# A decoder layer on one core: the FFN's down-projection by Strassen's seven products, in three batches of the contraction

## The chip, the cores and the metric

The kernel runs on one core of a Trainium2 chip. Times are device microseconds (us) of one execution. The profile is that of one execution, taken by the hardware profiler. Engines: PE (TensorE, matmuls), PEld (its weight loads), DVE (VectorE), ACT (ScalarE), POOL (GpSimd), SP (SyncE, which only issues DMAs here). SPq, ACTq and so on are the queues from which DMAs and semaphore instructions are issued.

## What is computed

A decoder layer with retention, differential attention and a gated MLP, on 1024 positions and 16 meta tokens, model width 1024, FFN width 2816, float32. Only its end is touched:

```python
    u = rmsnorm(h, norm2_w[l])
    up = causal_dwconv(u @ w_up[l].astype(dt), conv_w[l], conv_b[l])
    a, b = jnp.split(up, 2, axis=-1)
    h = h + (jax.nn.silu(a) * b) @ w_down[l].astype(dt)
```

w_up is 1024 x 5632, w_down 2816 x 1024. All is kept transposed: channels on the 128 partitions, positions along a row.

## The kernel before

Every matmul is done in float32r with both operands split: h is a cast to float32r on ACT, l the rest (x - h) by a subtraction. A product is three matmuls, (wh, xh), (wh, xl), (wl, xh), written out in product() (L1186). The subtractions are put in a list by low_later() and written out on DVE by lows() (L1138) a few steps later; those of the weights whose name stands in self.pooled go to POOL (L1144).

From last_ret_out on, the program is recorded by hand: each engine runs its instructions in the order of the code. What an engine waits for, all behind it on the engine waits for too.

**Up-projection.** It already goes by Strassen's algorithm in Winograd's form. Block f (0 to 21; NF = 22) makes the rows f (part a) and NF + f (part b) of the up-projection, for 1032 positions in two halves of 516. The seven products are named A F B E H G D, in that order on PE; each runs over four row tiles of 128, in two pieces of 258 columns, into one double bank of PSUM (four double banks in turn). B is added to A's bank, D to E's. Around them: A is copied by ACT (L1716), A + B too (L1730); DVE forms "sw" (L1625, after F), "su" (L1631, after H), mid() (L1635, which reads E's bank before D adds to it), and the results ub (L1640, after G) and ua (L1645, after D). The weights of the products come from five loads of 256 KB (s1 s3 a b d), two of them completed by an adding DMA on POOL (L1549) and two sums on DVE ("S" L1556, "T" L1558); seven casts and subtractions make the operands for block f + 1 during block f, in the order A, S F, B, H, E, T G, D.

**Activation.** Behind block f come, two blocks later, the convolution and the gate: ACT starts it (L1594), DVE adds the taps (L1600, four for each part), ACT does Silu (L1603), DVE multiplies twice (L1605), and SP stores the 128 x 1024 result to DRAM (L1607).

**Down-projection.** Eleven passes of two row tiles each; a pass reads two activations back (L1799), splits them (ACT L1806, DVE L1138), and for each of eight row tiles m of the output does two products of 1024 columns in two banks. DVE adds the bank to the residual h[m] in SBUF (L1787), which in the last pass goes out in halves (L1789):

```python
                self.product([(ps[:, :512], 0, 512), (ps[:, 512:], 512, 512)], [(w(o + i), (gh[i], gl[i])) for i in range(2)])
                for cs in [slice(0, 512), slice(512, SEQ)] if last else [slice(0, SEQ)]:
                    V.tensor_add(h[m][:, cs], h[m][:, cs], ps[:, cs])
```

The residual lies in DRAM (self.hs) before and is loaded at the end of block 21. Large tiles come from one pool of 34 (big()).

## Time and profile before

| | |
|---|---|
| median of 3 runs | 2491.41 us (2488.54 to 2492.39) |
| profiled execution, its own time | 2491.43 us |
| its span (first to last instruction) | 2489.7 us |
| busy: PE, DVE, ACT, POOL | 2447.4, 1705.7, 1041.8, 431.1 us |
| clock granted to PE, mean | 0.999 |
| HBM read, written | 199.55 MB, 58.12 MB |

A row of the trace groups equal instructions that follow each other: start, length, engine, line, operation, tiles, count, and in brackets how long the engine was idle before and what ended that. The length of a group of x2 or x4 is from the first start to the last end; neighbours overlap a little, so I go by the spacing of starts. Numbers of buffers are left out of the names: u is ua, d a bank of PSUM, wr a raw tile of weights, wh and wl its two parts, b a large tile.

### The profile page before, as it was taken

The page shows a single profiled execution, that of the slowest core. Times are in us where ns is not written, and L with a number is a line of the kernel's source. Part 1 is how long each engine was busy: PE and PEld are TensorE (multiplying, and loading weights), DVE is VectorE, ACT ScalarE, POOL GpSimd, SP SyncE. Part 2 cuts the span into 40 slices and gives each one's busy share as a digit, 9 for nine tenths or more (in the row PEclk, how much of TensorE's full clock was granted, in tenths as well). Part 3 has the DMA queues.
Part 4 walks back from the last instruction along what each step waited for, and adds up shares of the span by engine and source line. Part 5 has one row for each costly group of instructions (what it writes and reads, how often), then busy time and mean ns, then how long its engine had stood idle before and what let it go on. Part 6 is the DMA issues. An engine that isn't in the chain of part 4 may idle for free. (4 is left out here: it accounts for less than half of the span.)

```text
span 2489.7 us, 42767 instructions
## 1 busy us (share of the span) xinstructions
PE 2447.4 (98%) x16186; PEld 2355.1 (95%) x16186; DVE 1705.7 (69%) x3625; ACT 1041.8 (42%) x2106; POOL 431.1 (17%) x412
## 2 busy tenths in 40 slices
...
DMA packets 193582, 279.82 MB, mean 112 GB/s; under 512 B 29160, under 2 KB 111712, under 8 KB 193376
## 3 DMA queue, kind: packets, MB, share of 16 engines
...
HBM read 199.55 MB, written 58.12 MB: 103 GB/s over the span
## 5 line engine op out<-in xcount | busy, mean ns | idle before, releaser
L180 PE MATMUL acc<-b,wh 128*128 128x342 f32 (+2 forms) x4672 | 1122.2, 323 | 5.2 <-DVE ev L630 3.7
L180 PEld LDWEIGHTS acc<-b,wh 128*128 128x128 f32 x4672 | 802.9, 189 | 7.3 <-issue 4.0
L180 PE MATMUL acc<-b,wl 128*128 128x342 f32 (+2 forms) x2336 | 749.4, 321 | 0.0
L1186 PE MATMUL d<-b,wh 128*128 128x258 f32 (+3 forms) x3936 | 732.0, 305 | 8.5 <-DVE b L1138 3.3
L1186 PEld LDWEIGHTS d<-b,wh 128*128 128x128 f32 x3936 | 585.4, 189 | 41.5 <-DVE b L1138 4.5
L1186 PE MATMUL d<-b,wl 128*128 128x258 f32 (+3 forms) x1968 | 440.3, 305 | 2.4 <-POOL wl L1144 1.4
L180 PEld LDWEIGHTS acc<-b,wl 128*128 128x128 f32 x2336 | 441.2, 189 | 0.0
L1186 PEld LDWEIGHTS d<-b,wl 128*128 128x128 f32 x1968 | 318.7, 189 | 19.1 <-POOL wl L1144 2.6
L1142 ACT CAST wh<-wr 128x512 fp32r<-128x512 f32 x246 | 144.4, 616 | 164.9 <-DVE wr L1556 79.4
L1144 POOL TENSOR_TENSOR wl<-wr,wh 128x512 fp32r<-128x512 f32 x84 | 114.9, 1385 | 512.0 <-ACT wh L1142 498.0
L233 ACT CAST wh<-wr 128x512 fp32r<-128x512 f32 x192 | 113.3, 618 | 172.8 <-PE acc L180 157.2
L630 DVE TENSOR_TENSOR ev<-acc,b 128x342 f32<-128x342 f32 (+2 forms) x141 | 72.2, 513 | 157.3 <-PE acc L180 149.9
L1787 DVE TENSOR_TENSOR b<-b,d 128x1024 f32<-128x1024 f32 (+1 forms) x96 | 107.3, 1129 | 73.7 <-PE d L1186 71.1
L719 ACT ACTIVATE b<-b,sm 128x272 f32<-128x272 f32 (+7 forms) x128 | 101.1, 790 | 107.3 <-DVE sm L718 84.0
L711 DVE CUSTOM_DVE_ANT_0 b<-sc,consts 128x144 f32<-128x144 f32 (+6 forms) x224 | 105.9, 504 | 42.2 <-PE sc L180 41.2
L252 POOL TENSOR_TENSOR b<-b,b 128x512 fp32r<-128x512 f32 x64 | 86.2, 1348 | 209.2 <-ACT b L247 180.9
L234 DVE TENSOR_TENSOR wl<-wr,wh 128x512 fp32r<-128x512 f32 x154 | 105.6, 703 | 22.1 <-ACT wh L233 22.0
L247 ACT CAST ah<-sc 128x512 fp32r<-128x512 f32 (+2 forms) x144 | 67.3, 468 | 115.5 <-PE sc L736 92.9
L1138 DVE TENSOR_TENSOR wl<-wr,wh 128x512 fp32r<-128x512 f32 x162 | 106.9, 684 | 10.4 <-ACT wh L1142 10.4
L252 DVE TENSOR_TENSOR al<-sc,ah 128x512 fp32r<-128x512 f32 (+2 forms) x144 | 77.3, 538 | 44.8 <-ACT ah L247 43.9
L596 POOL TENSOR_TENSOR sh<-sh,b 128x346 f32<-128x346 f32 (+1 forms) x42 | 43.3, 1032 | 354.6 <-DVE sh L594 354.6
L180 PE MATMUL sc<-b,b 128*128 128x346 f32 (+9 forms) x528 | 103.2, 316 | 0.1
...
## 6 DMA issues: line engine op xcount, KB each, us to landing
wr<-w_in SPq DMA_DIRECT2D x164, 256.0 KB
wr<-w_up SPq DMA_DIRECT2D x118, 256.0 KB
...
b<-d SPq DMA_DIRECT2D x256, 64.0 KB
...
wr<-w_up POOLq DMA_DIRECT2D x44, 256.0 KB, 4.7
```

The source lines that it names most:

```text
L180: self.E.matmul(out, lhsT=l, rhs=r, start=start, stop=stop)
L233: self.A.copy(h, raw)
L234: (self.G if el == "G" else self.V).tensor_sub(l, raw, h.bitcast(F32))
L252: (self.V if el == "V" else self.G).tensor_sub(dl, src, dh.bitcast(F32))
L630: V.tensor_mul(o[:, :n], ps[:, :n], self.rb[:, cs])
L711: V.tensor_tensor_reduce(out=sc_[:m, a0:a0 + sz], in0=ps[:m, :sz], in1=mk, scale=1.0, scalar=3e38, op0=ALU.add, op1=ALU.min, accum_out=sm[ ...
L719: A.activation(sc_[:m, :n], sc_[:m, :n], AF.Exp, bias=mx, scale=-1.0, accum_out=sm[:m, 10 + c:11 + c])
L1138: self.V.tensor_sub(l, x, h.bitcast(F32))
L1142: self.A.copy(w[0], raw)
L1144: self.G.tensor_sub(w[1], raw, w[0].bitcast(F32))
L1186: self.E.matmul(o[:, :n], lhsT=l, rhs=x[:, t0:t0 + n], start=f, stop=e, skip_group_check=more)
L1787: V.tensor_add(h[m][:, cs], h[m][:, cs], ps[:, cs])
```

## The change

The down-projection goes by the same seven products. The 22 row tiles of the contraction are taken in three batches of 8, 8 and 6; a batch is four blocks (22 to 25, 26 to 29, 30 to 33) that run in the loop of the up-projection's blocks, with 4, 4 and 3 row tiles per product and halves of 512 positions. Each block gives two of the output's eight row tiles.

keep() takes the place of the activation's store: from each activation it makes what the seven operands A, H, E, F, G or B, D, F, G, H need (one subtraction on DVE, in the second half of a batch also a negation on ACT) and writes it to DRAM, five transfers of 256 KB; what two activations give together is added by the transfer (issued from POOL), the rest is stored from ACT's queue. One block before a batch begins, fetch() loads the operands from ACT's queue, one after each product (forms(0) to forms(6)), in two tiles of 1024 columns (1024 and 512 in the last batch), and two steps later finish() casts each tile on ACT and puts its subtraction in DVE's list. The blocks of the first two batches add their two rows to the residual in DRAM by adding transfers from POOL (add()); those of the last batch load it (rows()), add it on DVE and store the output.

```diff
+    def stage_of(f): return 0 if f < NF else 1 + (f - NF) // 4
+    @staticmethod
+    def tiles_of(f): return 3 if f >= NF + 8 else 4
+    def pair_of(self, f):
+        if f < NF:
+            return self.a["w_up"][f], self.a["w_up"][NF + f]
+        i = 8 * ((f - NF) // 4) + (f - NF) % 4
+        return self.a["w_down"][i], self.a["w_down"][i + 4]
...
+    def keep(self, f, o, x):
+        s, n = 1 + f // 8, 3 if f >= 16 else 4
+        k, second = (f - 8 * (s - 1)) % n, f - 8 * (s - 1) >= n
+        lo, hi, a, b = o[:, :512], o[:, 512:SEQ], x[:, :512], x[:, 512:SEQ]
+        if second:
+            self.V.tensor_sub(a, hi, lo)
+            self.A.activation(b, hi, AF.Copy, scale=-1.0)
+        else:
+            self.V.tensor_sub(a, lo, hi)
+        for name, t in zip(*(("BDFGH", (lo, hi, hi, a, b)) if second else ("AHEFG", (lo, hi, a, a, a)))):
+            if (s, name) not in self.part:
+                self.part[s, name] = self.dram([P, 2048])
+            d = self.part[s, name][:, 512 * k:512 * k + 512]
+            if second and name in "FGH":
+                self.nc.gpsimd.dma_start(out=d, in_=t, accum_op=ALU.add)
+            else:
+                self.A.dma_start(out=d, in_=t)
+    def fetch(self, name, f):
+        s, n = self.stage_of(f), 512 * self.tiles_of(f)
+        cs = [slice(0, 1024), slice(1024, n)]
+        self.coming[name] = [self.big()[:, :c.stop - c.start] for c in cs]
+        for t, c in zip(self.coming[name], cs):
+            self.A.dma_start(out=t, in_=self.part[s, name][:, c])
+    def finish(self, name, f):
+        out = self.ops[self.stage_of(f), name] = []
+        for t in self.coming.pop(name):
+            h, l = self.big(F32R), self.big(F32R)
+            c = slice(0, t.shape[1])
+            self.A.copy(h[:, c], t)
+            self.low_later(l[:, c], t, h[:, c])
+            out.append((h, l))
+            self.lows(1)
...
     def quad_product(self, ps, f, name, more=False):
         w = self.wq[f].pop(name)
-        outs = [(ps[:, 512 * g:512 * g + 512], t0, n) for g, (t0, n) in enumerate(self.PIECES)]
-        self.product(outs, [((w[0][:, k, :], w[1][:, k, :]), self.xs(name, k)) for k in range(4)], not more, True, more)
+        outs = [(ps[:, 512 * g:512 * g + 512], t0, n) for g, (t0, n) in enumerate(self.PIECES if f < NF else [(0, 512)])]
+        self.product(outs, [((w[0][:, k, :], w[1][:, k, :]), self.xs(name, k, f)) for k in range(self.tiles_of(f))], not more, True, more)
...
-            self.acts.append(self.dram([P, SEQ]))
-            self.S.dma_start(out=self.acts[f], in_=o[0][:, :SEQ])
+            self.keep(f, o[0], o[1])
...
+        def add(f):
+            m = (f - NF) % 4
+            for t, r in ((ua[f], m), (ub[f], m + 4)):
+                self.nc.gpsimd.dma_start(out=self.hs[r][:, 8:], in_=t[:, :SEQ], accum_op=ALU.add)
+        def rows(f):
+            h = [self.big() for _ in range(2)]
+            for t, r in zip(h, ((f - NF) % 4, (f - NF) % 4 + 4)):
+                self.S.dma_start(out=t[:, :SEQ], in_=self.hs[r][:, 8:])
+            return h
+        def out(f, r, t, i):
+            c = slice(512 * i, 512 * i + 512)
+            self.S.dma_start(out=self.a["out"][(f - NF) % 4 + 4 * r][:, c], in_=t[:, c])
...
+        end = NF + 12
+        for f in range(2, end):
+            pro, n = f < self.PRO, wid(f)
+            final = f >= NF + 8
+            fresh = f + 1 in (NF, NF + 4, NF + 8)
+            begun = f in (NF, NF + 4, NF + 8)
+            todo = iter([] if f == end - 1 else ["E", "HSF", "T", "GD"] if f + 1 < self.PRO else ["A", "SF", "B", "H", "E", "TG", "D"])
+            self.pooled = "EFHGD" if f + 1 < self.PRO else "BED" if f < NF - 1 else 'BEDG'
+            start, taps, mul = act.pop(f - 2) if f < NF + 2 else 3 * [lambda *a: None]
             def w():
                 self.lows()
-                for n in next(todo, ""):
-                    self.weights(f + 1, n)
+                for i in next(todo, ""):
+                    self.weights(f + 1, i)
...
+            def forms(i):
+                names = "AFBEHGD"
+                if fresh:
+                    if i > 1:
+                        self.finish(names[i - 2], f + 1)
+                    self.fetch(names[i], f + 1)
+                elif begun and i < 2:
+                    self.finish(names[i + 5], f)
             if not pro:
                 ua[f] = self.work()
-                st[f] = ua[f][:, 516:1032]
+                st[f] = ua[f][:, n:2 * n]
                 pt = self.dbl()
                 self.quad_product(pt, f, "A")
-                A.copy(bd(st[f]), d2(pt))
+                A.copy(bd(st[f]), d2(pt, f))
                 w()
                 taps(1)
-            if last:
-                self.queue = [self.a["w_down"][i] for i in range(NF)]
-                self.request()
-                self.request()
+                forms(0)
...
             up_f(f)
             if pro:
                 taps(1)
             w()
+            forms(1)
             if not pro:
                 taps(0)
                 self.quad_product(pt, f, "B", True)
-                A.copy(bd(ua[f][:, :516]), d2(pt))
+                if final:
+                    h = rows(f)
+                    V.tensor_add(ua[f][:, :512], pt[:, :512], h[0][:, :512])
+                    out(f, 0, ua[f], 0)
+                else:
+                    A.copy(bd(ua[f][:, :n]), d2(pt, f))
                 w()
-            if last:
-                self.down_fetch(0)
-            if self.PRO <= f + 2 < NF:
+            forms(2)
+            if self.PRO <= f + 2 < end:
                 self.quad_loads(f + 2)
             up_e(f)
-            if last:
-                self.arrive()
+            forms(3)
             if pro and f == 3:
                 w()
             up_h(f)
             mid(f)
+            if final:
+                V.tensor_add(ub[f][:, 512:SEQ], ub[f][:, 512:SEQ], h[1][:, 512:SEQ])
+                out(f, 1, ub[f], 1)
+                V.tensor_add(su[f], su[f], h[1][:, :512])
+                V.tensor_add(sw[f], sw[f], h[0][:, 512:SEQ])
             if pro:
                 taps(0)
             if not pro or f == 2:
@@ -1747,65 +1842,30 @@
             if f == 2:
                 w()
             mul()
-            if self.PRO <= f + 2 < NF:
+            forms(4)
+            if self.PRO <= f + 2 < end:
                 self.sum_d(f + 2)
-            if last:
-                down = self.down_split()
             w()
             up_g(f)
-            act[f - 1] = self.activation(f - 1, ua[f - 1], ub[f - 1])
-            act[f - 1][0](1)
+            forms(5)
+            if final:
+                out(f, 1, ub[f], 0)
+            if f - 1 < NF:
+                act[f - 1] = self.activation(f - 1, ua[f - 1], ub[f - 1])
+                act[f - 1][0](1)
             w()
             up_d(f)
-            act[f - 1][0](0)
+            if final:
+                out(f, 0, ua[f], 1)
+            if f - 1 < NF:
+                act[f - 1][0](0)
+            if f >= NF and not final:
+                add(f)
+            forms(6)
             w()
             for names in todo:
                 self.weights(f + 1, names)
             self.lows()
-            if last:
-                for _ in range(8):
-                    load_h()
-        h = done
-        f = NF - 1
...
-        for p in range(NF // 2):
-            gh, gl = down
...
     def down_blocks(w):
-        w = w.reshape(11, 2, P, 2, 4, P)
-        return np.ascontiguousarray(w.transpose(0, 3, 2, 4, 1, 5)).reshape(22, P, 8, P)
+        w = w.reshape(NF, P, 8, P)
+        b = np.zeros((3, 8, P, 8, P), w.dtype)
+        for i in range(2):
+            b[i] = w[8 * i:8 * i + 8].transpose(2, 1, 0, 3)
+        b[2, :, :, :3] = w[16:19].transpose(2, 1, 0, 3)
+        b[2, :, :, 4:7] = w[19:].transpose(2, 1, 0, 3)
+        return np.ascontiguousarray(b.reshape(24, P, 8, P))
```

On PE the inner pattern changes. The first matmuls of the down-projection before (x2: the two halves of a double bank with the same weights; b are the two parts of an activation):

```order
L1186 MATMUL d_26044<-b_25949,wh_25907 128x512 x2
L1186 MATMUL d_26044<-b_25950,wh_25907 128x512 x2
L1186 MATMUL d_26044<-b_25949,wl_25908 128x512 x2
L1186 MATMUL d_26044<-b_25952,wh_25907 128x512 x2
L1186 MATMUL d_26044<-b_25953,wh_25907 128x512 x2
```

and those of block 22 now:

```order
L1186 MATMUL d_26219<-b_26006,wh_25925 128x512
L1186 MATMUL d_26219<-b_26007,wh_25925 128x512
L1186 MATMUL d_26219<-b_26006,wl_25926 128x512
L1186 MATMUL d_26219<-b_26006,wh_25925 128x512
L1186 MATMUL d_26219<-b_26007,wh_25925 128x512
```

One bank of 512 columns per row tile, so every tile of weights is used for one matmul of each kind.

On ACT, before, from the Silu of block 20 to the first copy of block 21 (the copy is L1716; between are casts of weights and the start of an activation):

```order
L1603 ACTIVATE b_25542<-b_25542 128x1024
L1142 CAST wh_25713<-wr_25405 128x512
L1594 ACTIVATE b_25743<-b_25467,cols 128x512 x2
L1142 CAST wh_25747<-wr_25413 128x512
L1594 ACTIVATE b_25775<-u_25305,cols 128x512 x2
L1142 CAST wh_25779<-wr_25411 128x512
L1716 COPY u_25783<-d_25784 128x516
```

and now the same place one block later, the end of block 21 up to the first copy of block 22 (L1805); L1535 are the casts of finish() for the operands E and H, L1528 the loads of fetch():

```order
L1535 CAST b_26154<-b_26060 128x1024
L1535 CAST b_26157<-b_26061 128x1024
L1528 DMA b_26161<-d_21377 128x1024
L1528 DMA b_26162<-d_21377 128x1024
L1651 ACTIVATE b_26165<-b_25811,cols 128x512 x2
L1142 CAST wh_26170<-wr_25757 128x512
L1651 ACTIVATE b_26199<-u_25649,cols 128x512 x2
L1535 CAST b_26202<-b_26117 128x1024
L1535 CAST b_26205<-b_26118 128x1024
L1142 CAST wh_26214<-wr_25755 128x512
L1805 COPY u_26218<-d_26219 128x512
```

The copy stands behind the operands' casts; the two rows left out are further loads. Ahead of this piece stand the Silu, the negation, two stores of keep() and the casts of B.

On DVE, now, in block 22 (L1138 on b: the operands G and D, on wl: weights; L1657 the taps; L1686 "sw", L1613 "S", L1692 "su", L1697 mid()):

```order
L1657 SCALAR_TENSOR_TENSOR b_26165<-b_25811,cols,b_26165 128x512 x4
L1138 TENSOR_TENSOR wl_26234<-wr_26021,wh_26233 128x512
L1138 TENSOR_TENSOR b_26241<-b_26161,b_26240 128x1024
L1686 TENSOR_TENSOR sw_26261<-u_26218,d_26248 128x512
L1138 TENSOR_TENSOR b_26245<-b_26162,b_26244 128x1024
L1613 TENSOR_TENSOR wr_26021<-wr_26021,wr_26017 128x512
L1138 TENSOR_TENSOR wl_26266<-wr_26021,wh_26265 128x512
L1138 TENSOR_TENSOR b_26269<-b_26209,b_26268 128x1024
L1657 SCALAR_TENSOR_TENSOR b_26199<-u_25649,cols,b_26199 128x512 x4
L1138 TENSOR_TENSOR b_26273<-b_26210,b_26272 128x1024
L1692 TENSOR_TENSOR su_26334<-d_26321,sw_26261 128x512
L1697 TENSOR_TENSOR b_26336<-su_26334,d_26308 128x512
```

Before, the four subtractions of b are not there; between the two groups of taps stand "sw", a weight's subtraction and "S", and after the second group a weight's subtraction, "su" and mid().

## Rows read from the trace of the kernel before

**Rows 1.** The page's first part: busy us (share of the span) x instructions of each engine.

```profile
PE 2447.4 (98%) x16186; PEld 2355.1 (95%) x16186; DVE 1705.7 (69%) x3625; ACT 1041.8 (42%) x2106; POOL 431.1 (17%) x412
```

**Rows 2.** Busy time of the engines in stretches of 50 us: the start of the up-projection's blocks, their steady part, the down-projection. Columns: stretch, its length, busy us of PE, PEld, DVE, ACT, POOL (x instructions), granted clock of PE, busy share of the DMA engines, GB/s.

```profile
1850.00:1900.00 50.00, 46.04 (x373) 44.93 (x372) 45.33 (x56) 24.19 (x36) 20.03 (x17) 1.00 0.51 128
2150.00:2200.00 50.00, 50.00 (x418) 50.00 (x417) 36.75 (x52) 23.62 (x38) 15.55 (x14) 1.00 0.46 112
2250.00:2300.00 50.00, 50.00 (x218) 40.59 (x217) 42.46 (x48) 13.57 (x19) 0.00 (x0) 1.00 0.43 154
```

**Rows 3.** Groups of matmuls by line and shape: the two of 512 columns at L1186 (x count | busy us, mean ns of one | idle before).

```profile
L1186 PE MATMUL d<-b,wh 128*128 128x512 f32 x704 | 190.9, 392 | 0.0
...
L1186 PE MATMUL d<-b,wl 128*128 128x512 f32 x352 | 109.8, 393 | 0.0
```

**Rows 4.** PE in order of time, in the down-projection: start, length, matmuls.

```profile
2255.99 0.62 PE L1186 MATMUL d<-b,wl 128*128 128x512 f32 x2
2256.45 1.09 PE L1186 MATMUL d<-b,wh 128*128 128x512 f32 x4
2257.37 0.63 PE L1186 MATMUL d<-b,wl 128*128 128x512 f32 x2
```

**Rows 5.** The same in the input projection, where each tile of weights is used for one bank at a time.

```profile
100.16 0.32 PE L180 MATMUL acc<-b,wl 128*128 128x346 f32 x1
100.31 0.48 PE L180 MATMUL acc<-b,wh 128*128 128x346 f32 x2
100.63 0.32 PE L180 MATMUL acc<-b,wl 128*128 128x346 f32 x1
```

**Rows 6.** DVE in order of time, its last row: the two adds behind the last matmul.

```profile
2485.09 1.28 DVE L1787 TENSOR_TENSOR b<-b,d 128x512 f32<-128x512 f32 x2 [1.47 <-PE d L1186]
```

**Rows 7.** ACT in order of time, in block 20 and at the start of block 21.

```profile
2203.95 0.59 ACT L1716 COPY u<-d 128x516 f32<-128x516 f32 x1 [3.57 <-PE d L1186]
...
2212.75 1.06 ACT L1603 ACTIVATE b<-b 128x1024 f32<-128x1024 f32 x1 [1.43 <-DVE b L1600]
2213.71 0.60 ACT L1142 CAST wh<-wr 128x512 fp32r<-128x512 f32 x1
...
2216.16 1.52 ACT L1594 ACTIVATE b<-u,cols 128x512 f32<-128x512 f32 x2
2219.99 0.62 ACT L1142 CAST wh<-wr 128x512 fp32r<-128x512 f32 x1 [2.32 <-DVE wr L1558]
2224.18 0.59 ACT L1716 COPY u<-d 128x516 f32<-128x516 f32 x1 [3.57 <-PE d L1186]
2229.91 0.59 ACT L1730 COPY u<-d 128x516 f32<-128x516 f32 x1 [5.14 <-PE d L1186]
```

**Rows 8.** DVE in order of time, in block 20 and at the start of block 21.

```profile
2206.86 0.69 DVE L1625 TENSOR_TENSOR sw<-u,d 128x516 f32<-128x516 f32 x1 [1.66 <-PE d L1186]
...
2208.80 3.91 DVE L1600 SCALAR_TENSOR_TENSOR b<-u,cols,b 128x512 f32<-128x512 f32 x4
...
2215.47 0.69 DVE L1631 TENSOR_TENSOR su<-d,sw 128x516 f32<-128x516 f32 x1 [2.16 <-PE d L1186]
...
2216.81 1.29 DVE L1605 TENSOR_TENSOR b<-b,b 128x512 f32<-128x512 f32 x2
2218.02 0.68 DVE L1138 TENSOR_TENSOR wl<-wr,wh 128x512 fp32r<-128x512 f32 x1
...
2221.24 0.69 DVE L1645 TENSOR_TENSOR u<-sw,d 128x516 f32<-128x516 f32 x1 [1.34 <-PE d L1186]
...
2222.45 2.98 DVE L1600 SCALAR_TENSOR_TENSOR b<-b,cols,b 128x512 f32<-128x512 f32 x4
```

**Rows 9.** What it takes a queue to issue a DMA (SP and POOL in order of time: a load of 256 KB, a store of 512 KB twice, eight loads of 512 KB; two adding transfers of POOL), and the page's row for those adding transfers (256 KB each, median us from issue to landing).

```profile
1894.78 2.09 SPq L1128 DMA_DIRECT2D wr<-w_up  x2
1896.92 0.42 SPq L1607 DMA_DIRECT2D d<-b  x1
...
2238.39 0.32 SPq L1607 DMA_DIRECT2D d<-b  x1
2238.76 5.06 SPq L1697 DMA_DIRECT2D b<-d  x8
...
1891.17 1.83 POOL L1549 DMA_DIRECT2D wr<-w_up  x2
...
wr<-w_up POOLq DMA_DIRECT2D x44, 256.0 KB, 4.7
```

**Rows 10.** The front, blocks 2 to 4: the multiplies of the first two activations on DVE, the first copy of block 4 on ACT, and the matmul behind it.

```profile
1859.85 3.81 DVE L1605 TENSOR_TENSOR b<-b,b 128x512 f32<-128x512 f32 x2 [2.34 <-ACT b L1603]
...
1875.12 2.40 DVE L1605 TENSOR_TENSOR b<-b,b 128x512 f32<-128x512 f32 x2 [1.13 <-ACT b L1603]
...
1882.23 0.58 ACT L1716 COPY u<-d 128x516 f32<-128x516 f32 x1
...
1882.87 0.51 PE L1186 MATMUL d<-b,wh 128*128 128x258 f32 x2 [2.03 <-ACT u L1716]
```

**Rows 11.** Groups by line and shape from 2225 on: the split of one activation of 1024 columns (x count | busy us, mean ns of one | idle before).

```profile
L1806 ACT CAST b<-b 128x1024 fp32r<-128x1024 f32 x22 | 23.0, 1049 | 99.5 <-DMA b<-d 99.5
...
L1138 DVE TENSOR_TENSOR b<-b,b 128x1024 fp32r<-128x1024 f32 x22 | 26.1, 1220 | 3.0 <-ACT b L1806 2.9
```

**Rows 12.** The columns of rows 2, for 4 us in which the residual and the first activations are loaded.

```profile
2244.00:2248.00 4.00, 4.00 (x19) 3.25 (x18) 3.25 (x4) 0.00 (x0) 0.00 (x0) 1.00 1.02 418
```

109 lines of the change are left out of this document (39 added, 70 removed).

## The prediction

> **What bounds the kernel now.** The page's first part comes first: TensorE (PE) is busy 98% of the span, VectorE (DVE) 69%, ScalarE (ACT) 42% [rows 1]. An average says little, so I read the stretches. In the up-projection's steady part (2150 to 2200) and in the down-projection (2250 to 2300) PE has no idle time at all at a granted clock of 1.00, so there the time is the number of matmuls times their spacing; only around 1850 to 1900, where the up-projection starts, does PE lose 4 us in 50, with DVE at 45 [rows 2]. What the change removes from PE is therefore time, as long as nobody makes PE wait instead.
>
> **The matmuls.** Down-projection before: 704 + 352 = 1056 matmuls of 512 columns [rows 3], one group of six every 1.38 us (2255.99 to 2257.37), 0.23 us each, 242.9 us in all [rows 4]. After: twelve blocks of seven products; a product over n row tiles is 3n matmuls of 512 columns. n is 4, 4 and 3, so 4 x 7 x 3 x (4 + 4 + 3) = 924, at 0.23 us 212.5 us. Gain: 132 x 0.23 = 30.4 us. A tile of weights now serves one bank instead of two. That should cost nothing: the input projection at 100 us has the same pattern (wh, wh, wl, one bank each) and needs 0.16 us for 346 columns, 0.144 us of streaming at 2.4 GHz plus the same 0.017 us that 512 columns show over their 0.213 [rows 4, 5].
>
> **The end.** Now the last matmul is followed by two adds of 512 columns, 1.28 us [rows 6], and the output's transfer; after, by one add. I take 0.6 us off.
>
> **The steady up-projection.** A block lasts 20.23 us (one copy of product A to the next), so a product lasts 2.89 us [rows 7]. keep() gives DVE one subtraction (0.61 us by the spacing of the two multiplies) where DVE is idle over 4 us a block in waits for PE: "su", "sw" and "u" each begin on PE's time [rows 8]. Its two or five stores are on ACT, whose queue stops until DVE has multiplied. By the rows of the block that starts at 2203.95: the multiplies end at 2218.0, the subtraction at 2218.6, and five stores at 0.42 us, which is what a store of 512 KB takes on SP [rows 9], bring ACT to 2220.1. Behind them stand a cast, a pair of activations, a cast, a pair (4.0 us from 2213.71 to the end of the pair begun at 2216.16) and a last cast of 0.5, so ACT is free at 2224.6 and the copy of the next A ends at 2225.1 instead of 2224.7. PE needs it only for product B, a product after 2224.2, at 2227.1. I take nothing; the cover is 2.0 us, and each 0.1 us more per store eats 0.5 of it.
>
> **The front.** At 1882.87 PE already waits 2.03 us for just that copy, with ACT behind [rows 10]. In blocks 2 and 3 the multiplies end late (1863.6 and 1877.5), and the casts and activations that stand behind the Silu before would move behind five stores: about 2.5 us later at 1875, plus a wait for stores to land before a buffer is reused. Bounds 0 (the lag is absorbed) and 6; I take 3 us, lost for good, since PE has no idle time behind it to win back.
>
> **The first change of stage (blocks 21 and 22).** Here the down-projection's operands are made: seven, each of two tiles of 1024 columns, with a cast on ACT (0.99 us) and a subtraction on DVE (1.17 us) per tile [rows 11]; ten tiles in block 21, four in 22. DVE's block costs 36.75 / 50 of 20.23 = 14.9 us now [rows 2]; ten lows of 1.17 make 26.6 us (keep's 0.6 is paid by a low of the weights that goes to POOL). So the lag has to show somewhere, and I follow the order of the instructions on ACT and DVE, on the axis of before, where block 21 starts at 2221.3 (its copy of A at 2224.18, less a product).
> First ACT. It ends the copy of B at 2230.4 [rows 7], a cast at 2230.9, A's two at 2232.9 (0.5 and 0.99 us each). F's fetch waits behind a cast that waits for the sum S (2208.8 + 20.2 = 2229.0, where the slow taps begin [rows 8]), so it lands at about 2233.5 (some 4.5 us later, as POOL's transfers [rows 9]), F's casts end at 2235.5, then a cast and the Silu at 2237. DVE, held by two tiles' lows, does "su", the mid subtraction and another low before the multiplies, which end at 2240.6. Two stores end at 2241.4. Then, in order: two casts of B (2243.4), one weight, two of E (2245.9), a pair of activations, a weight, a pair (2249.4), two of H (2251.4), a weight, and only then the copy of block 22's first product, done at 2252.5. Product B of block 22 accumulates in the same bank and would start at 2241.4 + 2 x 12 x 0.23 = 2246.9. PE waits 5.6 us.
> Then DVE. It has H's second low at 2252.7, a pair of taps to 2255.7, then a weight's low, G, "sw", G, the weight sum S at 2259.9. ACT's next cast waits for S, so D's tiles come at 2262.4; DVE then does a low, D, the four slower taps (3.92 us [rows 8]), D, "su" and the mid subtraction, at 2268.9. Product D writes into the bank that the mid subtraction reads. PE, through with G at 2263.5, waits 5.4 us. Together 11.0 us. Lower bound 4, if tiles arrive early and DVE's taps all take 0.75 us; upper 20, if each of 14 fetches also holds ACT by 0.63 us (eight loads of 512 KB in 5.06 us on SP [rows 9]). Block 23 has no operands to make and catches up.
>
> **The other two changes of stage.** No activations run there. ACT has 5 x 2 x 0.99 + 7 x 0.52 + 1.1 = 14.6 us of work, DVE 11.7 + 3 + 3.3 = 18 us, against 19.3 us of PE. By the same walk ACT is through its chain 21.4 us after the block's start, before the copy's product ends at 22.1, and PE needs the copy at 24.8: a slack of 2.9 with the copy's 0.5. Lower bound 0. The bytes are tighter: 7.3 MB of operands, 1.8 MB of weights and 1 MB added to DRAM are 10.1 MB, 24 us at the 418 GB/s that the bursts at 2244 reach [rows 12]; but D may land in the next block. Upper bound 5 each; I take 1 each.
>
> **Hidden elsewhere.** The adding stores and the adds of the residual go out on POOL, which is busy about 15.6 of 50 us [rows 2], 0.9 us an issue [rows 9]; each block adds at most three issues, 2.7 us. No row shows an adding transfer into DRAM. The nearest is the one into SBUF (4.7 us to landing [rows 9]). What reads them comes at least three blocks (43 us) later, so between 0 and ten times that price nothing waits. More DRAM writes in the up-projection, 0.8 MB per block, add 40 GB/s to 112 [rows 2].
>
> **A rule weighed.** ACT has issued no DMA so far, so the trace can't say whether an issue stops its casts; SP's rows give only the price, 0.32 to 1 us [rows 9]. The Trainium skill (Perfetto Trace Analysis, section "DMA Instruction — HWDGE (DVE, Sync)") says that the sequencer itself waits for the semaphores and is free only when all descriptors are made; work already handed to the engine is not stopped. By that the wait for DVE in keep() holds all of ACT, as I have counted it; and the fetches are free only while ACT has a backlog. By its strict reading, with no backlog, the sum would be the second rival's.
>
> **Sum.** Against the profiled execution, 2491.43 us by its own time (span 2489.7, 1.7 us around it; the median of the runs is 2491.41): 2491.4 - 30.4 - 0.6 + 3 + 11 + 2 = 2476.4 us.
>
> **Rivals.** (1) The stage changes are hidden. For: products B and D wait only because of the queues' order, and ACT has 58% idle. Against: the walk above. 2491.4 - 31 + 0 to 8 = 2460 to 2468.
> (2) ACT's issues stand in line: each fetch of 512 KB costs ACT its 0.63 us. For: SP's loads stand back to back at that price. Against: ACT is backlogged there and should have casts handed over. Seven pairs are 8.8 us on the first change; on the others 8.8 less ACT's 2.9 of slack, 5.9 each: 2476.4 - 2 + 8.8 + 11.8 = 2495.0. It decides against the change where 42 issues less 5.8 us eat the 17 us that are left, from 0.54 us per issue; at 0.9 us, POOL's price, the changes cost 12.6 and twice 12.6 - 2.9, and the steady blocks with five stores (11 of them) lose (0.9 - 0.42) x 5 - 2.0 = 0.4 us each: 2476.4 - 2 + 12.6 + 2 x 9.7 + 4.4 = 2511.
> (3) Transfers bound the changes: operands land 5 us late at the second and third, and 3 us at the first: 2476.4 + 8 + 3 = 2487. For: 10.1 MB against 418 GB/s; against: the end of the fetch isn't needed until a block later.
> (4) The matmuls don't get 0.23 us with weights used once; then the gain shrinks by 0.9 us per ns: at 0.25 us, 2495. Against: rows 5.
>
> **How the numbers follow.** My forecast (2470 to 2483) 0.47; (1) 0.20; (2) 0.18; (3) 0.12; (4) 0.03. The predicted time is the forecast's, 2476. A measurement of this kernel tells about 0.2% (5 us) from no change, so faster ends at 2486.4: all of the forecast and (1), half of (3): 0.73. Within 0.2%, 2486.4 to 2496.4: half of (3), a part of (2) and (4): 0.14. Slower: the rest of (2): 0.13. The range 2463 to 2496 leaves out the lowest of (1) and the upper half of (2), some 0.15.
>
> **What would show it.** Right: 924 matmuls of 512 columns at 0.23 us; PE without idle time in blocks 5 to 20; a wait of PE for ACT's copy and one for DVE's mid subtraction after 2240, 4 to 8 us each, and under 3 us at the later changes. Wrong: PE waits for ACT's copies throughout (the store's price), waits of 5 us or more at the second and third change (issues or transfers), or none at the first. What would undo the forecast most is a price of ACT's issues over 0.54 us.

## The result, and the profile after

The changed kernel takes 2511.7 us (median of 4, 2509.97 to 2516.47) against 2491.9 of the kernel before beside it: ratio 1.0085, 95% interval 1.0067 to 1.0102: slower by 0.85%, clear of the spread. The forecast was 2476.4, the range 2463 to 2496. The profiled execution took 2511.67 us.

The page of the changed kernel, parts 1 and 3 (queues: packets, MB, share of the 16 engines' time), and three windows (us, busy us and instructions of PE, PEld, DVE, ACT, POOL, then granted clock, busy share of the transfer engines, GB/s):

```profile
PE 2431.2 (97%) x16054; PEld 2336.6 (93%) x16054; DVE 1737.6 (69%) x3665; ACT 1091.3 (43%) x2197; POOL 559.6 (22%) x531
q0 software_dynamic: 22608, 53.52, 12.3%
2150.00:2200.00 50.00, 49.02 (x405) 48.68 (x404) 41.73 (x55) 21.25 (x34) 18.97 (x17) 1.00 0.63 155
2250.00:2300.00 50.00, 35.21 (x133) 27.65 (x132) 41.67 (x45) 23.02 (x34) 18.94 (x17) 0.83 0.75 186
2300.00:2350.00 50.00, 41.76 (x174) 33.31 (x175) 24.17 (x30) 16.46 (x25) 21.79 (x21) 0.95 0.96 229
```

Before, PE was busy 2447.4 us [rows 1] and had no idle time from 2150 to 2200 and from 2250 to 2300 [rows 2]. Now it does less work, but stands still for 15 of the 50 us from 2250, at a granted clock of 0.83, and the transfer engines are full from 2300 to 2350 (0.96). The longest waits, from PE's timeline (in brackets how long PE stood, and for what):

```profile
1869.16 1.20 PE L1186 MATMUL d<-b,wh 128*128 128x258 f32 x4 [3.90 <-DVE b L1697]
1882.57 0.74 PE L1186 MATMUL d<-b,wh 128*128 128x258 f32 x4 [2.17 <-ACT u L1805]
2257.89 1.22 PE L1186 MATMUL d<-b,wh 128*128 128x512 f32 x2 [7.79 <-ACT u L1805]
2277.40 1.19 PE L1186 MATMUL d<-b,wh 128*128 128x512 f32 x2 [5.55 <-DVE b L1697]
2347.58 1.22 PE L1186 MATMUL d<-b,wh 128*128 128x512 f32 x2 [6.98 <-DVE b L1697]
2360.55 0.73 PE L1186 MATMUL d<-b,wh 128*128 128x512 f32 x2 [2.20 <-ACT u L1805]
2374.47 0.70 PE L1186 MATMUL d<-b,wh 128*128 128x512 f32 x2 [2.56 <-DVE b L1697]
2443.77 0.73 PE L1186 MATMUL d<-b,wh 128*128 128x512 f32 x2 [2.28 <-ACT u L1805]
2457.69 0.81 PE L1186 MATMUL d<-b,wh 128*128 128x512 f32 x2 [3.75 <-DVE b L1697]
```

L1805 is the copy of product A, L1697 the mid subtraction. The length of the group behind a wait tells the clock: a pair of 512 columns takes 0.70 to 0.73 us at full clock and 1.19 to 1.22 at the lower of its two levels, a four of 258 columns 0.74 and 1.20. So the front (the first blocks of the up-projection), the first change of stage (2257, 2277), the second (2347 to 2374) and the third (2443, 2457) all wait, not only the first change.

**The account.** I cut each trace at the copies of A and set the stretches against what PE alone needs: 19.43 us for a block of 84 matmuls (block 27 takes 19.44), so 0.2313 us per matmul. What a stretch takes beyond that is called its loss. "Front" runs from ACT's last table load, ahead of the first Silu, to the copy of block 21, less the 366.7 us of the kernel before; the three changes are blocks 21 to 23, 24 to 27, and 28 to the last copy, less 59.1, 77.7 and 81.9 us. Blocks 5 to 20 took 324.2 us (323.7 before). The loss is 8.1 + 19.6 + 16.0 + 12.1 = 55.8 us, against the 31 us won; 24.8 us slower by this sum, of which 4.9 don't show, because the untouched part ahead was that much shorter in this execution:

```profile
1852.54 1.28 ACT L1660 ACT_TABLE_LOAD   x1
```

and, of the kernel before,

```profile
1857.46 1.28 ACT L1603 ACT_TABLE_LOAD   x1
```

All runs (the ratio is to runs of the kernel before on the same chip; the columns of loss, in us, come from one profile each; a stage that an edit doesn't touch moves by up to 3 us in them, and the second change, 16.0 in the changed kernel, lies at 8.0 to 11.9 in e1, e9 and e11, whose edits end ahead of it. So a fall in the second column says little by itself; the medians and the sums of stages say more):

| run | median us | ratio (95%) | front | first | second | third |
|---|---|---|---|---|---|---|
| changed kernel | 2511.7 | 1.0085 (1.0067-1.0102) | 8.1 | 19.6 | 16.0 | 12.1 |
| e1_stores_sp | 2522.5 | 1.0129 (1.0113-1.0146) | 19.1 | 23.8 | 10.4 | 13.9 |
| e2_plain_store | 2505.5 | 1.0062 (1.0045-1.0079) | 6.7 | 19.1 | 8.7 | 8.2 |
| e3_warm | 2515.2 | 1.0098 (1.0083-1.0113) | 8.2 | 22.3 | 13.4 | 11.5 |
| e4_lows_pool | 2532.0 | 1.0166 (1.0151-1.0181) | 9.0 | 28.5 | 19.2 | 16.6 |
| e5_resid | 2519.1 | 1.0119 (1.0097-1.0142) | 7.6 | 23.3 | 16.7 | 10.4 |
| e6_late_stores | 2517.4 | 1.0110 (1.0091-1.0128) | 5.2 | 21.4 | 16.1 | 12.6 |
| e7_half_fetch | 2505.4 | 1.0056 (1.0041-1.0071) | 9.3 | 20.5 | 6.6 | 9.8 |
| e8_fewer_lows | 2505.7 | 1.0058 (1.0043-1.0073) | 8.4 | 17.2 | 11.2 | 11.6 |
| e9_own_tile | 2503.0 | 1.0045 (1.0028-1.0062) | 0.9 | 20.3 | 8.0 | 15.2 |
| e10_finish_later | 2512.1 | 1.0091 (1.0074-1.0109) | 8.7 | 20.8 | 12.7 | 11.5 |
| e11_no_taps | 2500.8 | 1.0039 (1.0024-1.0055) | 7.2 | 10.2 | 11.9 | 12.5 |
| e12_partials | 2566.1 | 1.0305 (1.0289-1.0320) | 7.6 | 19.7 | 9.3 | 53.6 |
| e13_all_out | 2475.4 | 0.9937 (0.9919-0.9954) | 0.9 | 4.4 | 2.3 | 5.8 |
| e14_fetch_ahead | 2494.2 | 1.0009 (1.0000-1.0019) | 0.9 | 19.6 | 7.5 | 8.2 |
| e15_first_plain | 2519.8 | 1.0113 (1.0097-1.0129) | 0.9 | 20.4 | 8.3 | 31.2 |
| e16_both | 2511.6 | 1.0079 (1.0062-1.0097) | 0.9 | 19.8 | 3.2 | 25.6 |
| e17_mid_first | 2497.0 | 1.0019 (1.0010-1.0028) | 0.9 | 17.6 | 6.4 | 8.2 |
| e18_three_ahead | 2500.1 | 1.0028 (1.0019-1.0036) | 0.9 | 16.9 | 9.3 | 8.8 |

### The profile page after: what moved, and what is told of

The parts are those of the page before. It is cut to its first block, busy times and chain, and to the rows that moved or that the text cites. A ratio compares the mean times of both kernels' runs of the same rounds, so it can differ in the third digit from the quotient of the medians.

```text
span 2509.9 us, 42988 instructions
## 1 busy us (share of the span) xinstructions
PE 2431.2 (97%) x16054; PEld 2336.6 (93%) x16054; DVE 1737.6 (69%) x3665; ACT 1091.3 (43%) x2197; POOL 559.6 (22%) x531
## 5 line engine op out<-in xcount | busy, mean ns | idle before, releaser
L1186 PE MATMUL d<-b,wh 128*128 128x258 f32 (+3 forms) x3848 | 743.8, 306 | 45.5 <-DVE b L1697 25.9
L1186 PEld LDWEIGHTS d<-b,wh 128*128 128x128 f32 x3848 | 574.6, 191 | 80.9 <-ACT u L1805 17.0
L1186 PE MATMUL d<-b,wl 128*128 128x258 f32 (+3 forms) x1924 | 456.5, 306 | 4.0 <-POOL wl L1144 3.5
L1186 PEld LDWEIGHTS d<-b,wl 128*128 128x128 f32 x1924 | 313.6, 191 | 20.7 <-POOL wl L1144 5.7
L1144 POOL TENSOR_TENSOR wl<-wr,wh 128x512 fp32r<-128x512 f32 (+1 forms) x130 | 188.7, 1527 | 502.0 <-ACT wh L1142 497.2
L1142 ACT CAST wh<-wr 128x512 fp32r<-128x512 f32 (+1 forms) x286 | 165.3, 606 | 281.7 <-DVE wr L1613 154.9
L233 ACT CAST wh<-wr 128x512 fp32r<-128x512 f32 x192 | 113.3, 618 | 174.7 <-PE acc L180 159.0
L1138 DVE TENSOR_TENSOR wl<-wr,wh 128x512 fp32r<-128x512 f32 (+1 forms) x156 | 119.2, 778 | 36.6 <-ACT wh L1142 35.5
L234 DVE TENSOR_TENSOR wl<-wr,wh 128x512 fp32r<-128x512 f32 x154 | 107.0, 712 | 22.1 <-ACT wh L233 22.0
L1138 DVE TENSOR_TENSOR b<-b,b 128x1024 fp32r<-128x1024 f32 (+3 forms) x88 | 95.0, 1093 | 38.3 <-ACT b L1535 23.1
```

The source lines that it names most:

```text
L233: self.A.copy(h, raw)
L234: (self.G if el == "G" else self.V).tensor_sub(l, raw, h.bitcast(F32))
L1138: self.V.tensor_sub(l, x, h.bitcast(F32))
L1142: self.A.copy(w[0], raw)
L1144: self.G.tensor_sub(w[1], raw, w[0].bitcast(F32))
L1186: self.E.matmul(o[:, :n], lhsT=l, rhs=x[:, t0:t0 + n], start=f, stop=e, skip_group_check=more)
```

## The experiments

### The front: e1, e6, e9

**e1.** keep()'s plain stores go out from SP.

```diff
-                self.A.dma_start(out=d, in_=t)
+                self.S.dma_start(out=d, in_=t)
```

> keep()'s plain stores go out from SP's queue instead of ACT's; the adding ones stay on POOL. Theory (ACT stands still in keep() until DVE has multiplied): the front loses its 8 us (waits of 3.90 and 2.17 us near 1869 and 1882, clock low for 7 us), and in block 22 the wait for the copy of A (7.79 us) shrinks by 2 to 4 us because ACT no longer issues 2 stores behind the multiplies there; together 2511.7 - 7 to 11 = 2501 to 2505. Rival (the front is late because DVE's own work in it grew by keep()'s subtraction, or stores share the transfer engines): the front's waits stay, 2510 to 2513. Second rival: SP's queue now waits for DVE ahead of the loads of weights, and POOL's sums and ACT's casts come late in the steady blocks: waits of PE between 1900 and 2240 and a time over 2515.

Slower by 11 us: the wait at 1869 falls to 0.86, but the next copy of A makes PE wait 7.93 (from 2.17), and the one in block 22 14.58. SP's loads of weights now stand behind the stores, which wait for DVE; in block 22 a cast of ACT waits 8.8 us for its weights. The second rival: 11.0 us more in the front, 5.2 in the steady blocks (329.5 us for blocks 5 to 20 against 324.2) and 4.2 at the first change.

**e6.** The stores stay on ACT, one and a half products later: keep() now stops (yield) ahead of them and goes on behind up_d().

```diff
-            self.keep(f, o[0], o[1])
+            self.kept = self.keep(f, o[0], o[1])
+            next(self.kept)
...
             up_d(f)
+            next(self.kept, None)
```

> Until block 20, keep()'s stores are issued from ACT one and a half products later, behind the casts of G and D and the first half of the next activation (L1651), so that ACT doesn't stand still for DVE's multiplies; from block 21 on as before. Theory (the front's 8 us come from ACT standing in keep() behind DVE, and from SP's queue when the stores were there): the waits of 3.90 and 2.17 us near 1869 and 1882 fall to at most 1 us each, as before the change (2.03), and no clock is lost there: 2511.7 - 4 to 7 = 2505 to 2508. Rival (DVE's own work in blocks 2 and 3 makes the front): the waits stay, 2510 to 2514.

No faster; the front still loses 5.2 us. ACT's timeline tells why; in the changed kernel, with DVE's taps that wait for it, then here:

```profile
1855.65 4.51 ACTq L1521 DMA_DIRECT2D d<-b  x5
1860.27 1.14 ACT L1142 CAST wh<-wr 128x512 fp32r<-128x512 f32 x2 [5.37 <-DMA d<-b]
1862.16 4.14 DVE L1657 SCALAR_TENSOR_TENSOR b<-b,cols,b 128x512 f32<-128x512 f32 x4 [3.40 <-ACT b L1651]
```

```profile
1865.11 3.66 ACTq L1523 DMA_DIRECT2D d<-b  x4
1870.73 1.52 ACT L1653 ACTIVATE b<-u,cols 128x512 f32<-128x512 f32 x2 [7.03 <-DMA d<-b]
```

In the changed kernel ACT has nothing else to do while it issues the five stores: its queue is taken from 1855.65 to 1860.16 (4.51 us, 0.90 each), the cast follows 0.1 us later, and the taps that wait for the activation behind it lead to the mid subtraction that PE waits for at 1869. In e6 the stores still stand ahead of the next activation's second pair (L1653), which now waits 7.03 us: four stores take the queue until 1868.77, and then the pair waits until 1870.7 for a store to *land*. That last 1.9 us fits a large tile that the stores still hold.

**e9.** keep()'s difference gets a tile of its own, so that the activation's second tile is free as soon as DVE has read it; the stores go to the end of the block, behind both pairs of the next activation.

```diff
-        lo, hi, a, b = o[:, :512], o[:, 512:SEQ], x[:, :512], x[:, 512:SEQ]
+        lo, hi, a, b = o[:, :512], o[:, 512:SEQ], self.xpool.tile([P, 512], F32, tag="ka", name=self.nm("ka")), x[:, 512:SEQ]
...
+        yield
...
+            next(self.kept, None)
             if f >= NF and not final:
```

> keep()'s difference goes into a tile of its own of 512 columns instead of into the activation's second tile, which is free again as soon as DVE has read it, and keep()'s stores are issued at the end of the block, behind the next activation's first steps. Theory (what ACT waited for in the front, 5.4 us and in the run with later stores 7.0 us marked as a store's landing, is a large tile that the stores still hold; the stores' place in the queue alone moves nothing): the waits of 3.90 and 2.17 us fall to at most 1 and 2.1, no clock is lost in the front, 2511.7 - 4 to 7 = 2505 to 2508. Rival (DVE is late by its own work, 0.6 us per block and the multiplies): the waits stay and the time is 2510 to 2514.

2503.0: the front's loss falls from 8.1 to 0.9 us, and the same pair of activations waits only 1.43 us, for DVE, ahead of the three stores that hold the new tile ("ka"):

```profile
1862.55 0.82 ACT L1654 ACTIVATE b<-u,cols 128x512 f32<-128x512 f32 x1 [1.43 <-DVE b L1665]
1863.53 3.40 ACTq L1524 DMA_DIRECT2D d<-ka  x3
```

The three stores are no shorter here (3.40 us), but nothing that PE needs stands behind them. So the front's loss comes from the stores on ACT's queue. Their place alone, as e6 has it, gives 2.9 us back; e9 gives 4.3 more, with a later place and a free tile at once. The tile alone was not run, and in the changed kernel's front the rows show the issues, not a wait for a tile.

### The first change: e3, e4, e8, e11, e10

**e3.** 32 and 22 idle matmuls fill PE's two waits in block 22.

```diff
+        WARM = {NF: (32, 22)}
...
+            for _ in range(WARM.get(f, (0, 0))[name == "G"]):
+                self.E.matmul(ps[:, 512:], lhsT=w[0][:, 0, :], rhs=self.xs(name, 0, f)[0], start=True, stop=True, skip_group_check=True)
```

> In block 22 alone PE gets matmuls that nobody reads, into the free half of a bank: 32 ahead of product B (32 x 0.23 = 7.4 us, where it waited 7.79) and 22 ahead of product D (5.1 us, where it waited 5.55). Theory (the waits lower the granted clock, and the 41 matmuls at 0.42 instead of 0.23 us behind them cost about 8 us on top): PE stays at 1.00 from 2250 to 2300, block 22 ends 5 to 8 us sooner, 2504 to 2507. Rival (the end of block 22 is set by DVE's and ACT's lag, and PE's slow matmuls lie in it): the clock stays up, but the wait ahead of D grows by what the first saved, 2510 to 2513. If the dummies themselves are in the way: over 2515.

The rival: the granted clock stays at 1.00, and nothing is won. Behind the 5.1 us of idle matmuls PE still waits 2.95, together 8 us where it waited 5.55.

```profile
2250.00:2300.00 50.00, 46.19 (x200) 36.56 (x200) 39.11 (x43) 25.34 (x35) 19.91 (x19) 1.00 0.74 185
2283.92 0.70 PE L1186 MATMUL d<-b,wh 128*128 128x512 f32 x2 [2.95 <-DVE b L1705]
```

**e4.** The first tile's subtraction goes to POOL.

```diff
+            if i == 0:
+                self.G.tensor_sub(l[:, c], t, h[:, c].bitcast(F32))
+            else:
+                self.low_later(l[:, c], t, h[:, c])
```

> Of each operand's two subtractions x - h at the changes of stage, the first tile's goes to POOL instead of DVE (21 of 42). Theory (DVE's lag makes the wait ahead of product D in block 22, and part of those marked with the subtraction L1697 in blocks 25, 26, 29 and 30): DVE loses 5 x 1.17 = 5.9 us in block 21, the wait of 5.55 us for the mid subtraction goes, and with it its 6.8 us of low clock; at the later changes only those parts of the waits that DVE makes; 2511.7 - 8 to 14 = 2498 to 2504. Rival (what is late is the transfer, and DVE only shows it): the later waits stay and block 22 alone gains, 2504 to 2508. Second rival: POOL, which also issues the adding transfers for the sums of weights, falls behind (a subtraction of 1024 columns may take it 2 us) and the weights come late: over 2512.

20 us slower, over the second rival's 2512. One subtraction on DVE that takes 1.2 us elsewhere lasted 12.57, over POOL's row of six subtractions (its first and last shown):

```profile
2262.13 12.57 DVE L1138 TENSOR_TENSOR b<-b,b 128x1024 fp32r<-128x1024 f32 x1 [2.29 <-ACT b L1535]
```

```profile
2262.56 1.60 POOL L1144 TENSOR_TENSOR wl<-wr,wh 128x512 fp32r<-128x512 f32 x1
...
2270.97 2.64 POOL L1537 TENSOR_TENSOR b<-b,b 128x1024 fp32r<-128x1024 f32 x1
```

The Trainium skill (SBUF — State Buffer, section "Who interferes with whom") says that a DVE instruction with two inputs in SBUF contends with a GpSimd instruction that reads SBUF, and calls this contention an exclusive lock. The trace agrees: DVE's subtraction, begun 0.4 us ahead of POOL's row, ends 1.1 us behind POOL's last. How the 20 us divide between such subtractions and late weights, the rival's reason, was not tried.

**e8.** The second tile's subtraction is left out.

```diff
-            self.low_later(l[:, c], t, h[:, c])
-            out.append((h, l))
+            if not out:
+                self.low_later(l[:, c], t, h[:, c])
+            out.append((h, l if not out else h))
```

> For the second tile of each operand the subtraction x - h is left out, and the product takes h in its place (the result loses precision); all transfers and casts stay. DVE is relieved of 21 subtractions, 5 x 1.17 = 5.9 us in block 21, without POOL taking any. Theory A (transfers bind all changes): block 22 gains under 3 us, later blocks nothing: 2507 to 2512. Theory B (DVE's lag binds the first change): the wait ahead of D in block 22 (5.55 us) goes, that for the copy of A shrinks by 1 to 3: 2511.7 - 6 to 9 = 2502 to 2506. Theory C (DVE binds all the changes): 2511.7 - 15 or more, under 2497.

The wait ahead of D falls to 2.10, as theory B has it, but that for the copy doesn't shrink (8.45), and the first change wins 2.4 us in all.

**e11.** DVE's taps of three activations are left out.

```diff
-                for i in (1, 0):
+                for i in (1, 0) if not 19 <= f < 22 else ():
```

> DVE's taps of the last three activations (blocks 21 to 23) are left out, 8 instructions and 6 to 8 us in each block; transfers, casts and operands' subtractions stay. Theory (the first change costs what DVE has too much: 26.6 us of work in a block of 20): block 22's waits of 7.8 and 5.6 us go, but for 2 to 4 us of the copy's that ACT makes by itself, and block 21's 9.8 us of loss shrink likewise: 2511.7 - 10 to 15 = 2497 to 2502, and nothing moves in blocks 25 to 31. Rival (transfers, or ACT's casts behind them, bind it): 5 us or less, 2507 to 2512.

The first change's loss falls from 19.6 to 10.2, the wait ahead of D is gone, a wait of 6.08 for the copy is left. The medians fall by 10.9 us. So with DVE's surplus goes half of this change's loss.

**e10.** Only the order: finish() later.

```diff
-                    if i > 1:
-                        self.finish(names[i - 2], f + 1)
+                    if 3 <= i < 6:
+                        self.finish(names[i - 3], f + 1)
...
-                elif begun and i < 2:
-                    self.finish(names[i + 5], f)
+                elif begun and i < 4:
+                    self.finish(names[i + 3], f)
```

> finish() comes a product later for A, F and B (three instead of two products after the fetch) and four or five later for E, H, G and D, which are then made at the beginning of the next block, behind the copy of A. No transfer, cast or subtraction is left out. Theory (the waits come from the order: the copy of A and the subtractions of PSUM stand in their queues behind casts and subtractions of operands that wait for their transfers): block 22's wait for the copy falls from 7.8 to 3 or less, the waits in blocks 25 and 29 fall by half, 2511.7 - 10 to 18 = 2494 to 2502. Rival (ACT and DVE have that much work, in whatever order, or the transfers that much to move): the waits only move to later products of blocks 22, 26 and 30, 2508 to 2514, or more where E or H then comes too late for its own product.

The wait for the copy falls to 3.08, as the theory has it, but four waits of 0.8 to 2.9 for E's and H's tiles take its place: the rival, no gain.

### The later changes: e2, e5, e7, e12

**e2.** add() stores instead of adding.

```diff
-                self.nc.gpsimd.dma_start(out=self.hs[r][:, 8:], in_=t[:, :SEQ], accum_op=ALU.add)
+                self.nc.gpsimd.dma_start(out=self.hs[r][:, 8:], in_=t[:, :SEQ])
```

> add()'s transfers of the first two batches' rows into the residual in DRAM store instead of adding (same queue, same count, same bytes; the residual and the sum over the batches are left out of the result). Theory (an adding transfer into DRAM holds the transfer engines far longer than a store; they are full from 2284 to 2340): the waits of blocks 25, 26, 29 and 30 (about 26 us lost there against the ideal) shrink to the 2 to 4 us that I had predicted for them, the engines' share in that stretch falls from about 1.0 to 0.7, and the time is 2511.7 - 15 to 22 = 2490 to 2497. Rival (the lag of DVE's subtractions and of ACT's casts makes those waits, as at the first change): nothing moves there, 2508 to 2513. In both, block 22 keeps its waits of 7.8 and 5.6 us.

6 us by the medians, not 15 to 22. The same window, 2284 to 2345, in both (queue q0 is POOL's; packets, MB, share of the engines), the changed kernel first:

```profile
q0 software_dynamic: 2618, 6.32, 61.9%
q1 hardware_dynamic: 2070, 3.75, 21.0%
```

```profile
q0 software_dynamic: 2853, 6.76, 50.1%
q1 hardware_dynamic: 2158, 3.93, 21.8%
```

A megabyte of POOL's queue costs 9.8% of the engines with the rows' adding transfers and 7.4% without them, one of q1's 5.6%. All queues together still take 0.89 of the engines (0.97 before), since more is moved in the window: 14.45 MB for 13.02. The rows' 512 KB land after 9.1 ("u") and 11.6 us ("b") adding, 7.3 and 7.8 storing.

**e7.** The second tile's transfer is left out.

```diff
-        for t, c in zip(self.coming[name], cs):
+        for t, c in zip(self.coming[name][:1], cs):
...
+            t = ts[0][:, c]
```

> fetch() loads only the first of an operand's two tiles, and finish() makes both pairs h, l from it: half of the operands' bytes (21 of 42 loads of 512 or 256 KB) are left out, all of ACT's casts and DVE's subtractions stay (the down-projection's result is wrong). Theory A (the transfers of the operands bind all three changes): ACT's waits for the fetched tiles go, the waits of blocks 25, 26, 29 and 30 fall under 3 us together, and block 22 loses at least half of its 13.3 us: 2511.7 - 22 to 32 = 2480 to 2490. Theory B (ACT's casts and DVE's subtractions bind the first change, as I had predicted, transfers only the later two): block 22 keeps 10 us or more, 2490 to 2500. Theory C (DVE everywhere): 2505 to 2512.

Neither A nor B alone: 6.3 us by the medians. The first change keeps all of its loss; the second's is 6.6 for 16.0 and the third's 2.3 less, but the second also moves in runs that don't touch it, so only the 6.3 us are shown. What stood at the second, ACT in the changed kernel:

```profile
2336.56 1.05 ACT L1535 CAST b<-b 128x1024 fp32r<-128x1024 f32 x1 [2.75 <-DMA b<-d]
2340.99 1.04 ACT L1535 CAST b<-b 128x1024 fp32r<-128x1024 f32 x1 [3.38 <-DMA b<-d]
2343.90 1.04 ACT L1535 CAST b<-b 128x1024 fp32r<-128x1024 f32 x1 [1.87 <-DMA b<-d]
```

The casts wait for the operands, DVE's subtractions for the casts, and the mid subtraction, behind them in DVE's queue, comes at 2346.84: PE's wait at 2347.58. The run leaves out half of ACT's issues too, but ACT stands idle for transfers here, not behind issues.

**e5** loads, adds and stores the rows by SP and DVE in all batches; **e12** stores them plainly and lets POOL add both sums in the last batch.

```diff
+            dst = self.a["out"][m][:, c] if f >= NF + 8 else self.hs[m][:, 8 + 512 * i:520 + 512 * i]
+            self.S.dma_start(out=dst, in_=t[:, c])
...
-            final = f >= NF + 8
+            final = f >= NF
```

> The blocks of the first two batches treat the residual as those of the last do: they load their two rows from SP's queue, DVE adds them, and SP stores; POOL's adding transfers of the rows are gone (the result is the same). Theory (what the storing run without adding gained, 6 us by the medians and 10 by the profiles, is the price of adding in DRAM): as fast as that run, 2500 to 2506, with the waits of blocks 25, 26 and 29 down by 2 to 6 us each. Rival (the transfer engines were simply full of bytes at that place, whoever moves them): the same bytes go through SP, so nothing is won, 2509 to 2514; if SP's queue, with loads and stores that wait for DVE, holds up the weights: over 2514.

```diff
-                self.nc.gpsimd.dma_start(out=self.hs[r][:, 8:], in_=t[:, :SEQ], accum_op=ALU.add)
+                self.nc.gpsimd.dma_start(out=self.total(f, r), in_=t[:, :SEQ])
...
+                for b in (NF, NF + 4):
+                    self.nc.gpsimd.dma_start(out=t[:, :SEQ], in_=self.total(b, r), accum_op=ALU.add)
...
+            if final and f + 1 < end:
+                ahead[f + 1] = rows(f + 1)
```

> The rows of the first two batches are stored from POOL's queue into tiles of their own in DRAM, without adding; the last batch's blocks load the residual a block ahead, and POOL adds the two partial sums to it by transfers into SBUF (four of 512 KB per block). The result is the same. Theory (the price of the adding transfers into DRAM is 6 us by the medians, as the run that stored without adding gave, and the last batch has room for 2 MB more per block): 2504 to 2508. Rival (the last batch's blocks, 14.5 us each, then wait for those sums, which take 5 us each and more beside the operands of the third change): blocks 30 to 33 lose 2 to 4 us each, 2510 to 2520.

Both rivals. e5 wins nothing at the later changes; PE waits 2.08 and 3.28 for POOL's part of the weights. In e12 DVE waits 40.3 us in the last batch for the rows, and PE up to 11.7 a block, far over the rival's 2 to 4. What makes the rows late is POOL: four adding transfers per block, the second sum of a row only when the first has landed, POOL and then DVE:

```profile
2449.51 1.80 POOL L1778 DMA_DIRECT2D b<-d  x2 [7.69 <-DMA b<-d]
2455.21 0.69 DVE L1831 TENSOR_TENSOR u<-d,b 128x512 f32<-128x512 f32 x1 [9.02 <-DMA b<-d]
```

### Everything at once, and repairs: e13 to e18

**e13** is e9 with the edits of e11, e7 and e2 together.

> Built on the run with the difference in a tile of its own (2503.0): the taps of the last three activations, the second tile's transfers and the adding of the rows are left out at once (the result is wrong). Theory (the changes of stage lose their 46 us to DVE's surplus, to the transfers and to the tiles that transfers hold, and to nothing else; each run that took one of them away showed the next behind it): blocks 21 to 31 lose less than 15 us against the ideal, 2478 to 2485, near the 2476 that I had predicted. If the gains simply add (11 for the taps, 6 for the transfers, 6 for the adding): 2480. Rival (something common to all, ACT's casts or the order of the queues, sets the changes): 2490 or more.

2475.4, 36 us under the changed kernel: all 55.8 us of loss but 13.4 are gone. At the second and third change, where no taps run, only the halved transfers and the plain stores differ from e9, and the two losses fall from 23.2 to 8.1 us together, more than these columns move by themselves. The largest wait left in blocks 21 to 33 is this one:

```profile
2250.50 0.73 PE L1187 MATMUL d<-b,wh 128*128 128x512 f32 x2 [2.79 <-ACT u L1812]
```

**e14** is e9 with the fetches begun two products earlier, **e15** e9 with the first batch stored plainly, **e16** both.

```diff
+                n = 2 if f > NF else 0
...
-                    self.fetch(names[i], f + 1)
+                    if i + n < 7:
+                        self.fetch(names[i + n], f + 1)
+                elif f + 2 in (NF + 4, NF + 8) and i >= 7 - 2:
+                    self.fetch(names[i - 7 + 2], f + 2)
```

> Built on the run with the difference in a tile of its own (2503.0): at the second and third change the fetches begin two products earlier (A's and F's behind the last two products of block 24 and 28), so that they have two products more to land; finish() stays where it is, nothing is left out. Theory (in blocks 25 and 29 the casts wait for transfers, and DVE's subtraction that frees E's bank stands behind them): the waits of blocks 25 and 29 (3.2 and 3.3 us, with their low clock) go, 2503 - 6 to 10 = 2493 to 2497. Rival (the engines of the transfers are full over the whole of blocks 23 to 26, by bytes, so that an earlier start only moves the congestion): 2500 to 2505. Second rival (the two operands hold 4 of the 6 spare tiles, and the blocks' own tiles wait): over 2506.

```diff
+                if f < NF + 4:
+                    self.nc.gpsimd.dma_start(out=self.total(r), in_=t[:, :SEQ])
...
+                self.S.dma_start(out=h[i + 2][:, :SEQ], in_=self.total(r))
...
+                    for i in (0, 1):
+                        V.tensor_add(h[i][:, :SEQ], h[i][:, :SEQ], h[i + 2][:, :SEQ])
```

> Built on the run with the difference in a tile of its own (2503.0): the first batch's rows are stored without adding into tiles of their own, only the second batch adds to them, and the last batch's blocks load residual and sums from SP's queue and add both on DVE (4 more instructions of 1024 columns in all per pair of blocks). The result is the same. Theory (adding takes longer than storing): blocks 23 to 25 win 3 to 5 us, the last batch loses under 1: 2498 to 2501. Rival (the last batch's loads, 2 MB per block and four large tiles, come late): 2504 or more; 10 us more if each of the last four blocks waits.

> The two edits before together. If both theories hold and add: 2489 to 2494, level with the kernel before (2491). If transfers' bytes set the later changes whatever their order and kind: 2500 to 2505.

e14 is level with the kernel before (1.0009), 8.8 us better than e9; by its profile the gain lies at the third change (15.2 to 8.2), while the second's wait stays (3.37 for 3.23). e15 wins nothing at the second change and loses 16 at the third, where DVE waits 3.9 and 3.4 us at a time for the rows; e16 likewise, though its second change loses only 3.2. In e15's first block of the last batch SP's row shows what the later of these loads had waited for, the load and then SP's wait (us in total, times, longest):

```profile
2443.74 0.32 SPq L1783 DMA_DIRECT2D b<-d  x1
SPq L1783 <- DMA d<-b: 10.8, 1, 10.8
```

It loads a row of the residual, to which no transfer adds in this run. What it waits 10.8 us for is the landing of POOL's adding transfer issued at 2431.82, 11.9 us later, which reads from a large tile: the load needs the tile.

**e17** is e14 with the mid subtraction of block 22 ahead of the slower taps, **e18** also begins the fetches three products earlier.

```diff
-                taps(0)
+                if f != NF:
+                    taps(0)
...
-            if pro:
+            if pro or f == NF:
                 taps(0)
```

> Built on the run with the fetches begun two products earlier (2494.2): in block 22 alone DVE does the slower four taps behind the mid subtraction instead of ahead of it; nothing is left out. Theory (product D of block 22 waits 7.96 us for the mid subtraction because DVE's queue has 4 us of taps ahead of it): that wait shrinks by 3 to 4 us, and PE has less of the low clock behind it: 2489 to 2492, level with or just under the kernel before. Rival (DVE has that much work in any order): the wait moves to block 23's products, 2493 to 2496.

> The run before, with the fetches of the second and third change begun three products earlier instead of two. If lateness of the transfers still makes the waits of 3.4 and 3.1 us there: 1 to 4 us less, 2486 to 2490, faster than the kernel before. If the six spare tiles are then all taken and the blocks' own tiles wait: 2 us or more above the run before.

The wait ahead of D falls as expected, in e14, then in e17:

```profile
2272.89 1.19 PE L1187 MATMUL d<-b,wh 128*128 128x512 f32 x2 [7.96 <-DVE b L1702]
```

```profile
2272.80 1.19 PE L1187 MATMUL d<-b,wh 128*128 128x512 f32 x2 [4.05 <-DVE b L1702]
```

but only 2 us of it reach the end of the first change, and the ratios are no better (1.0019 and 1.0028 against 1.0009). No version run here with all of its work gets under the kernel before.

## Why the prediction was wrong, step by step

- **The matmuls: right.** 0.2313 us each, and e13, with the suspects out, comes at 2475.4, where the forecast's 2476.4 had 16 us of loss and this run 13.4. The end, 0.6 taken: from the last matmul's end to the end of the span it is 4.6 us before (2485.06 to 2489.7) and 3.7 now (2506.18 to 2509.9), so 0.9.
- **Steady blocks: right in sum.** 0.5 us over blocks 5 to 20, with one wait of PE of 0.98 at 2172. The price of a store was not 0.42: five take 2.65 to 3.57 us of ACT's queue there. The cover of 2.0 us was enough for that.
- **ACT's issues: right for the fetches, not for the front's stores.** The fourteen fetches of the first change took 0.45 us on average (0.33 to 1.00), under the 0.54 from which the second rival decides. ACT casts meanwhile: the issue at 2233.60 lasts 1.21, the two casts begin at 2233.98. The rule that was weighed (the Trainium skill, Perfetto Trace Analysis, section "DMA Instruction — HWDGE (DVE, Sync)") has the sequencer free for its next instruction only when the descriptors are made. The trace agrees: in the front ACT stands idle for the 4.51 us of the five stores, so there its issues do stand in line, as the second rival has it, at 0.90 us each.

```profile
2226.91 0.81 ACTq L1528 DMA_DIRECT2D b<-d  x2
2233.60 1.21 ACTq L1528 DMA_DIRECT2D b<-d  x2
2233.98 2.00 ACT L1535 CAST b<-b 128x1024 fp32r<-128x1024 f32 x2
```

- **The front: the mechanism right, the loss mis-sized, 3 taken, 8.1 measured, over the upper bound of 6.** I put the lag down to five stores in ACT's queue, and that is what the rows show. Five cost 4.51 us where the walk had 2.1. PE's wait at this place was 0.86 us in the kernel before and is 3.90 now, 3.0 more; that this is the 3 I had taken is luck, with such a price per store. What the sum had no term for is the clock behind the wait: it is 0.78 from 1870 to 1880 now and was 1.00 there before. Before:

```profile
1871.23 0.72 PE L1186 MATMUL d<-b,wh 128*128 128x258 f32 x4 [0.86 <-DVE b L1635]
```

- **The first change: right places and engines, size off.** PE waits for the copy (7.8, I had 5.6) and for the mid subtraction (5.55, I had 5.4), the two steps of the walk. The loss is 19.6 instead of 11: these 13.3, another 1.6 at 2300, and 4.7 that I put down to matmuls at the lower clock level, again without a term in the sum (argued, not shown: with the clock up, e3, DVE's lag took their place). What the walk lacked on DVE stands in its rows:

```profile
2257.75 3.30 DVE L1138 TENSOR_TENSOR b<-b,b 128x1024 fp32r<-128x1024 f32 x1 [2.12 <-DMA d<-b]
2276.57 0.69 DVE L1697 TENSOR_TENSOR b<-su,d 128x512 f32<-128x512 f32 x1
```

  2.12 us for a tile that keep()'s adding transfer holds, and 3.30 instead of 1.17, while POOL subtracts from 2255.91 to 2259.97 (e4 shows how).
- **The other two changes: the step that failed.** 1 us each forecast, 5 the bound; 16.0 and 12.1 measured, 26 of the 40 us by which the sum of the losses is off. Two steps carried it. The first is "between 0 and ten times that price nothing waits", which looked only at who *reads* the sums. But a byte on POOL's queue takes the transfer engines a third longer when the rows are added than when they are stored (e2), and the operands' loads stand beside it on the same engines. And an adding transfer holds the tile that it reads *from* until it lands, 9 to 12 us (medians 9.1 and 11.6). At the third change DVE waits for such a tile, and PE's wait at 2457.69 is for the mid subtraction behind it:

```profile
2455.53 0.69 DVE L1138 TENSOR_TENSOR b<-b,b 128x512 fp32r<-128x512 f32 x1 [1.95 <-DMA d<-b]
```

  The second step divided 10.1 MB by a burst's 418 GB/s [rows 12], 24 us, already more than a block of 19.4, and took 1 us. With the engines full, the stretch at the second change moved 229 GB/s (2300 to 2350), since the operands' fetches share the engines with POOL's queue; at that rate 10.1 MB would take 44 us (an estimate). Rival (3) had the mechanism, with 8 us more than the forecast where there are 26. How much of the 26 is bytes, how much adding and how much held tiles was not separated; bytes and adding together are 15 (e13 against e9).
- **How they combine.** The changes have three causes of like size. Each taken away alone gave 6 to 11 us (e11, e7, e2: 23 in all, against the changed kernel), all three 27.6 (e13 against e9); the walk had priced one of them, DVE's surplus.

Open: what holds up the later blocks of e12 and e15 (held tiles, SP's place or the third change's bytes); why five stores take 4.51 us in the front and 2.65 to 3.57 later; what part of e9's gain is the tile's alone; and the spread of the second change in runs that don't touch it.
